# Emitting the inverses' rows later in a unit, and leaving three turns free behind the first loads of the output projection

## The chip, the cores and the metric

One core of a Trainium2 chip runs the whole program in one launch. The metric is the time on the device in microseconds (us); lower is better. The kernel before has a median of 3469.87 us over 3 runs (3465.22 to 3473.87).

## The reference

One layer of a bidirectional hybrid encoder, on 2048 tokens of width 1024 in float32. A normed input is projected; one half of the channels runs through a Mamba-2 SSD group, the other through an RWKV-7 group (8 heads of 64), both in both directions of time; the two outputs are concatenated and go through one output projection; a squared-ReLU MLP follows.

```python
proj = h @ w_in
y_ssd = ssd_bidir(...)                     # 512 channels
y_rwkv = rwkv7_bidir(...)                  # 512 channels
y = concatenate([y_ssd, y_rwkv], -1) @ w_out
...
mlp = square(relu(h @ w_fc)) @ w_proj
```

The RWKV group is a recurrence over time on a 64x64 state S of each head:

```python
s_kk = einsum('dbhvk,dbhk->dbhv', S, kk)
S = S * w + v (x) k - s_kk (x) (kk * a)    # (x): outer product
y = einsum('dbhvk,dbhk->dbhv', S, r)
```

The kernel computes it in chunks of 64 tokens. Within a chunk, the steps' dependence on each other is a triangular matrix of 64x64, and the kernel inverts it. This is the triangular inverse of the title.

## The kernel before

**Stages.** The program has three: the input projection with the preparation of both groups (to about 1040 us), the stage of the units (to about 2037 us), and the MLP. The change lies in the second alone.

**Units.** `phase_rwkv` works through 32 units. A unit is one pair of head groups at one step of time, 128 tokens of it forward and 128 backward; units with even and odd numbers belong to the two pairs of head groups, so a state waits for its own pair's unit before. The state of the recurrence goes from unit to unit through the chain: L999 multiplies on VectorE (DVE) in the preparation, in the chain the matmuls L1140, the copies L1158 (ScalarE, ACT) and L1159 (DVE), L1172 and L1169 (DVE). L1169 stands once in a unit, and the prediction counts the units in the trace from one L1169 to the next, 0 after the first.

**The jobs beside the chain.** `weave` runs the chain of unit u and, in between, a few generators for other units, each spread over a part of the unit: `prep(u+3)` over 0 to 0.3 of it, `inverse(u+2)` in 16 steps over IL to IH, `merge(u+1)` over 0.5 to 0.9, `finish(u-1)` over 0.4 to 1.0. What comes out is an order of emission. The Tile framework then schedules each engine's queue by its own model of time, with that order as the priority; the queues run in the order in which they were built.

**From prep to merge.** `prep` writes the triangular matrices to DRAM (L1040, ad<-at, on SP's queue). `inverse` loads them back in blocks of 16x16 (L1046, la<-ad), sets a unit matrix (L1049, ln), and runs 15 rows of two instructions, L1055 (ltmp<-ln,la) and L1056 (ln<-ln,ltmp). For an even-numbered unit all 15 stand on DVE, for an odd one on GpSimd (POOL). It stores the result (L1059, nd<-ln) and loads it back in another layout (L1062, ni<-nd). `merge` joins the blocks to 32x32 and 64x64: L1084, L1087, matmuls L1092, L1096, L1099, a transpose on DVE (L1103, n<-ip), copies on ACT (L1106, nm<-ip), matmuls L1112, and copies to nm again (L1124).

**The output projection as filler.** TensorE is kept busy with work from `out_pieces`, a generator. Where the chain or the merge leave TensorE waiting, `dense` adds a credit and takes pieces from the generator: a yield of DENSE is three matmuls of 128x512 (L828) and costs one credit; a yield of HELD ends the round and drops the credit left, so it is a turn in which no matmuls are put in. Up to unit 17 there are 8 such turns in a unit, and one tile of the output projection takes 8 pieces. Its first pass takes the SSD half (yS) of 16 tiles, its second the RWKV half (yR), which must wait for finished units (`FA` and `k.final`). `load` fetches a tile: h (L805), yr (L808, two buffers), scales yr on DVE in the first pass (L813), rounds it on ACT (L815, yh) and takes the rest on POOL (L817, yl). `products` runs the matmuls and adds them to h on DVE (L831 in the first pass, L833 in the second). Each tile's load is started one tile ahead.

**Norms.** `finish` normalizes the units' output (L1204 to L1240), with reciprocals on DVE (L1220).

Of the kernel before, what the change touches and what calls it, by code (L numbers as in the profile page):

```python
# [96 lines left out]
PGN = 2  # L97
PH = 0.3
ML = 0.5
IL = 0.0  # L100
KP = 0
DP = 0
PS = 0
IH = 0.4
RORD = (0, 4, 1, 5, 8, 2, 9, 6, 3, 7, 10, 11)
G0 = 2
EVB = {'u': 2, 'sg': 2, 'acc': 2, 'o': 4, 'ld': 3}
# [97 lines left out]
def ppc(k, name, j):  # L205
    c = _PP[name] + j
    return k.pp[:, c:c + 1]
# [564 lines left out]
DENSE, HELD, LAST, END = "dense", "held", "last", object()  # L772


def out_pieces(k):
# [3 lines left out]
    with ExitStack() as ctx:  # L779
# [23 lines left out]
        def load(t, ys, first):  # L803
            h = wk.tile([P, D], F32, name="h")
            nc.sync.dma_start(h, k.hD[t])  # L805
            yr = wk.tile([P, 4, P], F32, name="yr")
            for g in range(2):
                nc.sync.dma_start(yr[:, 2 * g:2 * g + 2], ys[g][:, :, P * t:P * t + P].rearrange("a p t -> p a t"))  # L808
            if first:
                rsb = wk.tile([P, 2, P], F32, name="rsb")  # L810
                nc.sync.dma_start(rsb, rsD[:, t].unsqueeze(0).broadcast_to([P, 2, P]))
                for c in range(4):
                    nc.vector.scalar_tensor_tensor(yr[:, c], yr[:, c], ppc(k, "ng", c), rsb[:, c // 2], ALU.mult, ALU.mult)  # L813
            yh = wk.tile([P, 4, P], F32R, name="yh")
            nc.scalar.copy(yh, yr)  # L815
            yl = wk.tile([P, 4, P], F32R, name="yl")
            nc.gpsimd.tensor_tensor(yl, yr, yh, ALU.subtract)  # L817
            return t, h, yh, yl

        def products(ops, first, rows=None):  # L820
            (wh, wl), (t, h, yh, yl) = k.wo, ops
            for hf in range(2):
                hs = slice(512 * hf, 512 * hf + 512)
                pt = k.psg.tile([P, 512], F32, name=k.psg_name)
                mm = [(yh, wh), (yh, wl), (yl, wh)]
                mm = [(y[:, c], w[:, c, hs]) for c in range(4) for y, w in mm]
                for i, (y, w) in enumerate(mm):
                    nc.tensor.matmul(pt, y, w, start=(i == 0), stop=(i == 11))  # L828
                    if i == 11:
                        if first:  # L830
                            nc.vector.scalar_tensor_tensor(h[:, hs], h[:, hs], ALPHA, pt, ALU.mult, ALU.add)  # L831
                        else:
                            nc.vector.tensor_tensor(h[:, hs], h[:, hs], pt, ALU.add)  # L833
                    if i + 1 in (CUTS[2 * (t % 2) + hf] if first else (3, 6, 9, 12)):
                        yield DENSE
            if rows:
                ln_apply(k, wk, h, *rows, k.eps[:, 0:1], True)
            nc.sync.dma_start(k.hD[t], h)
# [43 lines left out]
        yield  # L882
        order = [t for s in range(NT // 2, NT) for t in (NT - 1 - s, s)]
        ops = load(order[0], k.yS, True)
        for j in range(NT):
            nxt = load(order[j + 1], k.yS, True) if j + 1 < NT else None
            yield
            yield from products(ops, True)
            ops = nxt
# [36 lines left out]
def phase_rwkv(k):  # L926
    nc, tc, I = k.nc, k.tc, k.I
    with ExitStack() as ctx:
# [113 lines left out]
        def inverse(u):  # L1042

            la = sm.tile([P, 16, 16], F32, name="la")
            for q in range(2):
                nc.sync.dma_start(la[64 * q:64 * q + 64], dram(AD[u], 0, [1040, 64], [64, 16], [1, 16]))  # L1046
            ln = sm.tile([P, 8, 16], F32, name="ln")
            eng = nc.vector if SUBD and u % SUBD == 0 and u < SUBE else nc.gpsimd
            eng.tensor_copy(ln, idq)  # L1049
            tmp = sm.tile([P, 40], F32, name="ltmp")  # L1050
            for r in range(15):
                yield
                w, m = 15 - r, r // 2 + 1
                tv = tmp[:, 0:m * w].rearrange("p (m t) -> p m t", m=m)
                eng.tensor_tensor(tv, ln[:, 0:m, r:r + 1].broadcast_to([P, m, w]), la[:, r:r + 1, r + 1:16].broadcast_to([P, m, w]), ALU.mult)  # L1055
                eng.tensor_tensor(ln[:, 0:m, r + 1:16], ln[:, 0:m, r + 1:16], tv, ALU.subtract)  # L1056
            nd = k.dr.tile([64, 8, 2, 16], F32, name="nd", bufs=4)
            for q in range(2):
                nc.sync.dma_start(nd[:, :, q], ln[64 * q:64 * q + 64])  # L1059
            ni = NI[u] = sm.tile([P, 8, 16], F32, name="ni")  # L1060
            for h in range(2):
                nc.sync.dma_start(ni[hsl(h)], dram(nd, 8192 * h, [16, 64], [1024, 8], [1, 16]))  # L1062
# [187 lines left out]
        def weave(main, others):  # L1250
# [10 lines left out]
            for o in others:  # L1261
                if o[0] is not k.ssd:
                    while step(o[0], o[5]) is not END:
                        pass

        k.fill = out_pieces(k)
        k.credit = 0.0
        k.final = [0] * NT

        U = 2 * UN  # L1270
        for u in range(-AH, U):
# [8 lines left out]
            if 0 <= u + AH - 1 < U:  # L1280
                jobs.append((inverse(u + AH - 1), 16, IL, IH, PI))
            if u + AH < U:
# [212 lines left out]
```

## Time and profile before

| | us |
|---|---|
| median of 3 runs (lowest to highest) | 3469.87 (3465.22 to 3473.87) |
| profiled execution | 3477.84 |
| its span in the trace | 3476.0 |
| TensorE busy in it | 3162.8 (91%) |
| VectorE | 2035.9 (59%) |
| ScalarE | 1240.3 (36%) |
| GpSimd | 975.8 (28%) |
| mean granted TensorE clock | 0.936 |

How to read it: the shares are means over three stages with different limits. Below, PE is TensorE, PEld its weight loads, DVE VectorE, ACT ScalarE, POOL GpSimd, SP the engine whose queue issues the DMAs (SPq). The granted clock is the part of full speed at which TensorE was let run. A row of the timeline gives start, duration, engine, line, operation, out<-in and shape, and in brackets the idle time just ahead of it and what ended it.

### The profile page before, as it was taken

What the parts mean: (1) busy time and instruction counts of PE and PEld (TensorE: products, weight loads), DVE (VectorE), ACT (ScalarE), POOL (GpSimd) and SP (SyncE); (2) the same over time, 40 slices, a digit from 0 to 9 for tenths busy, and PEclk for the clock granted to TensorE, in tenths of its full rate; (3) what the DMA queues carried; (4) which work ended last, traced back from release to release, by engine and by line L of the source; (5) the groups of instructions that cost most, each with busy time, mean ns of one, the idle gap of its engine ahead of it and who ended that gap; (6) DMA issues with size and microseconds to landing.
All of it is one profiled execution on the core that took longest, in us unless ns stands there. A gap on an engine that the chain in (4) does not pass through costs nothing.

```text
span 3476.0 us, 62902 instructions
## 1 busy us (share of the span) xinstructions
PE 3162.8 (91%) x24551; PEld 2525.6 (73%) x24551; DVE 2035.9 (59%) x4186; ACT 1240.3 (36%) x2574; POOL 975.8 (28%) x1278
## 2 busy tenths in 40 slices
PE   5879989988876888888898889999999999999998
PEld 4767867766765666666666678888888788888886
DVE  7798457767675666565767554444444664444446
ACT  3556323433335454455655531122222222222221
POOL 0352134444553221223454551111111111111113
PEclk9989999999995899986978999999999999999999
DMA  5345356776777666656665552111111331111111
GB/s 206 132 158 179 122 148 190 210 214 189 214 226 198 158 170 157 161 158 171 171 164 156 151 189 91 49 49 46 47 49 49 103 109 49 49 49 49 49 49 61
DMA packets 630137, 446.70 MB, mean 129 GB/s; under 512 B 193456, under 2 KB 553552, under 8 KB 629840
## 3 DMA queue, kind: packets, MB, share of 16 engines
q1 hardware_dynamic: 629840, 442.69, 43.5%
q8 instruction: 193, 3.16, 0.4%
q14 instruction: 104, 0.85, 0.1%
HBM read 295.43 MB, written 147.14 MB: 127 GB/s over the span
## 4 chain that ended last, share of the span: by engine, by line
PE 58%; DMA 13%; DVE 13%; issue 4%; POOL 3%; SPq 2%; ACT 2%; DVEq 0%; POOLq 0%; ACTq 0%
PE ps L1362 7%; PE ps L1363 7%; PE ps L1364 7%; PE ps L1384 6%; PE ps L1382 6%; PE ps L1383 6%; PE psg L828 3%; DMA R<-rows 2%; PE psg L268 2%; PE psg L269 2%; PE psg L270 2%; PE ch L1140 2%; DMA la<-ad 1%; DMA ad<-at 1%; PE ps L1009 1%
## 5 line engine op out<-in xcount | busy, mean ns | idle before, releaser
L1388 DVE TENSOR_TENSOR acc<-acc,ps 128x512 f32<-128x512 f32 x464 | 318.2, 687 | 445.3 <-PE ps L1384 443.0
L1369 POOL TENSOR_TENSOR ul<-r,uh 128x512 fp32r<-128x512 f32 x128 | 171.1, 1338 | 1189.6 <-ACT uh L1368 1189.6
L1364 PE MATMUL ps<-hl,fh 128*128 128x512 f32 x1024 | 401.6, 392 | 0.0
L1363 PE MATMUL ps<-hh,fl 128*128 128x512 f32 x1024 | 401.5, 392 | 0.0
L1362 PE MATMUL ps<-hh,fh 128*128 128x512 f32 x1024 | 397.5, 393 | 0.6 <-DVE h L833 0.4
L1384 PE MATMUL ps<-ph,ul 128*128 128x512 f32 x1008 | 393.3, 390 | 0.0
L1383 PE MATMUL ps<-pl,uh 128*128 128x512 f32 x1008 | 393.0, 390 | 0.0
L1382 PE MATMUL ps<-ph,uh 128*128 128x512 f32 x1008 | 392.8, 390 | 0.0
L268 PE MATMUL psg<-hh,wh 128*128 128x512 f32 x864 | 357.2, 414 | 9.7 <-ACT u L287 8.9
L269 PE MATMUL psg<-hh,wl 128*128 128x512 f32 x864 | 354.8, 411 | 0.0
L270 PE MATMUL psg<-hl,wh 128*128 128x512 f32 x864 | 352.6, 409 | 1.4 <-DVE hl L238 1.4
L1350 ACT CAST ph<-wraw 128x1024 fp32r<-128x1024 f32 x63 | 63.3, 1051 | 531.2 <-PE ps L1384 527.8
L1362 PEld LDWEIGHTS ps<-hh,fh 128*128 128x128 f32 x1024 | 192.1, 188 | 43.6 <-DVE h L833 0.9
L1363 PEld LDWEIGHTS ps<-hh,fl 128*128 128x128 f32 x1024 | 192.3, 188 | 42.6
L1364 PEld LDWEIGHTS ps<-hl,fh 128*128 128x128 f32 x1024 | 192.2, 188 | 42.7
L1383 PEld LDWEIGHTS ps<-pl,uh 128*128 128x128 f32 x1008 | 189.4, 188 | 40.9
L1382 PEld LDWEIGHTS ps<-ph,uh 128*128 128x128 f32 x1008 | 189.1, 188 | 40.8
L1384 PEld LDWEIGHTS ps<-ph,ul 128*128 128x128 f32 x1008 | 189.3, 188 | 40.4
L268 PEld LDWEIGHTS psg<-hh,wh 128*128 128x128 f32 x864 | 169.5, 196 | 49.1 <-ACT u L287 10.1
L270 PEld LDWEIGHTS psg<-hl,wh 128*128 128x128 f32 x864 | 168.4, 195 | 39.6 <-issue 3.2
L269 PEld LDWEIGHTS psg<-hh,wl 128*128 128x128 f32 x864 | 169.3, 196 | 35.7 <-issue 2.3
L1366 ACT ACTIVATE r<-ps 128x512 f32<-128x512 f32 x128 | 76.8, 601 | 291.3 <-PE ps L1364 286.5
(294 smaller groups left out, 6182.6 us busy)
## 6 DMA issues: line engine op xcount, KB each, us to landing
h<-hD SPq DMA_DIRECT2D x64, 512.0 KB, 3.8
wraw<-in_w_fc_dram SPq DMA_DIRECT2D x64, 512.0 KB, 3.9
wraw<-in_w_proj_dram SPq DMA_DIRECT2D x64, 512.0 KB, 4.4
rk<-rk SPq DMA_DIRECT2D x64, 384.0 KB, 4.4
eD<-et SPq DMA_DIRECT2D x32, 514.0 KB, 2.7
E<-eD SPq DMA_DIRECT2D x64, 257.0 KB, 4.4
xs<-xg SPq DMA_DIRECT2D x64, 256.0 KB, 4.1
R<-rows SPq DMA_DIRECT2D x64, 256.0 KB, 4.4
```

The lines of the kernel that those rows point to most:

```text
L268: nc.tensor.matmul(pt, wh[:, c], hh[:, c], start=(c == 0), stop=False)
L269: nc.tensor.matmul(pt, wl[:, c], hh[:, c], start=False, stop=False)
L270: nc.tensor.matmul(pt, wh[:, c], hl[:, c], start=False, stop=(c == KC - 1))
L828: nc.tensor.matmul(pt, y, w, start=(i == 0), stop=(i == 11))
L1362: nc.tensor.matmul(pt, wh[:, c], k.hh[:, c, ns], start=(c == 0), stop=False)
L1363: nc.tensor.matmul(pt, wl[:, c], k.hh[:, c, ns], start=False, stop=False)
L1364: nc.tensor.matmul(pt, wh[:, c], k.hl[:, c, ns], start=False, stop=(c == KC - 1))
L1369: nc.gpsimd.tensor_tensor(ul[:, ns], r, uh[:, ns], ALU.subtract)
L1382: nc.tensor.matmul(pt, uh[:, ts], ph[:, hs], start=(i == 0), stop=False)
L1383: nc.tensor.matmul(pt, uh[:, ts], pl[:, hs], start=False, stop=False)
L1384: nc.tensor.matmul(pt, ul[:, ts], ph[:, hs], start=False, stop=(i == len(ops) - 1))
L1388: nc.vector.tensor_tensor(acc[j][:, hs], acc[j][:, hs], pt, ALU.add)
```

## The change

Two constants say over which part of a unit the rows of an inverse are emitted, IL and IH. They go from 0.0 and 0.4 to 0.25 and 0.7. And in `out_pieces`, behind the loads of the first tile of the first pass, three HELD yields are put in, so three turns pass without matmuls, and all of the first pass comes three turns (three eighths of a unit) later against the chain. Numbers, shapes and engines of instructions stay; their order changes. Behind the new lines, line numbers are 2 higher (L1055 is L1057).

```diff
-IL = 0.0
+IL = 0.25
...
-IH = 0.4
+IH = 0.7
...
         ops = load(order[0], k.yS, True)
+        for _ in range(3):
+            yield HELD
         for j in range(NT):
```

What the built queues show, at three places. First the steady part of the first pass. DVE's queue in a unit whose rows stand on DVE, before, from the multiplies L999 on (L1084 is the first step of the next merge):

```order
L999 TENSOR_TENSOR kr<-rk,E 128x2x128 x4
L1055 TENSOR_TENSOR ltmp<-ln,la 128x15
L831 SCALAR_TENSOR_TENSOR h<-h,psg 128x512
L1056 TENSOR_TENSOR ln<-ln,ltmp 128x15
L1055 TENSOR_TENSOR ltmp<-ln,la 128x14
L1103 STREAM_TRANSPOSE n_13436<-ip 128x256
L1056 TENSOR_TENSOR ln<-ln,ltmp 128x14
L1084 TENSOR_TENSOR dd<-ni,rc 128x256
L1055 TENSOR_TENSOR ltmp<-ln,la 128x26
L1056 TENSOR_TENSOR ln<-ln,ltmp 128x2x13
L1055 TENSOR_TENSOR ltmp<-ln,la 128x24
```

And after:

```order
L1001 TENSOR_TENSOR kr<-rk,E 128x2x128 x4
L1057 TENSOR_TENSOR ltmp<-ln,la 128x15
L1058 TENSOR_TENSOR ln<-ln,ltmp 128x15
L1057 TENSOR_TENSOR ltmp<-ln,la 128x14
L1058 TENSOR_TENSOR ln<-ln,ltmp 128x14
L1057 TENSOR_TENSOR ltmp<-ln,la 128x26
L1105 STREAM_TRANSPOSE n_13398<-ip 128x256
L1086 TENSOR_TENSOR dd<-ni,rc 128x256
L1058 TENSOR_TENSOR ln<-ln,ltmp 128x2x13
L1057 TENSOR_TENSOR ltmp<-ln,la 128x24
L1058 TENSOR_TENSOR ln<-ln,ltmp 128x2x12
```

The first row stands directly behind the multiplies in both; h's accumulation L831 leaves its place behind the first row, and the transpose (L1103, now L1105) comes one row step later.

The end of the same rows on DVE, before, from the addition L831 on:

```order
L831 SCALAR_TENSOR_TENSOR h<-h,psg 128x512
L1056 TENSOR_TENSOR ln<-ln,ltmp 128x5x6
L1016 TENSOR_TENSOR ra<-ps,rc 128x4x64 x2
L997 TENSOR_TENSOR bk<-bk_13962,E 128x2x128 x2
L1055 TENSOR_TENSOR ltmp<-ln,la 128x30
L1056 TENSOR_TENSOR ln<-ln,ltmp 128x6x5
L1055 TENSOR_TENSOR ltmp<-ln,la 128x24
L1056 TENSOR_TENSOR ln<-ln,ltmp 128x6x4
L1055 TENSOR_TENSOR ltmp<-ln,la 128x21
L1056 TENSOR_TENSOR ln<-ln,ltmp 128x7x3
L1055 TENSOR_TENSOR ltmp<-ln,la 128x14
```

And after, where the same stretch holds yr (L813):

```order
L1018 TENSOR_TENSOR ra<-ps,rc 128x4x64 x2
L1058 TENSOR_TENSOR ln<-ln,ltmp 128x6x4
L1057 TENSOR_TENSOR ltmp<-ln,la 128x21
L1058 TENSOR_TENSOR ln<-ln,ltmp 128x7x3
L813 SCALAR_TENSOR_TENSOR yr<-yr,pp,rsb 128x128 x2
L1057 TENSOR_TENSOR ltmp<-ln,la 128x14
L813 SCALAR_TENSOR_TENSOR yr<-yr,pp,rsb 128x128 x2
L1058 TENSOR_TENSOR ln<-ln,ltmp 128x7x2
L999 TENSOR_TENSOR bk<-bk_13943,E 128x2x128 x2
L1057 TENSOR_TENSOR ltmp<-ln,la 128x8
L1058 TENSOR_TENSOR ln<-ln,ltmp 128x8
```

yr stood beside the rows 7 and 8 before, further up; it stands around row 14 now, and fewer rows are left behind L997 (now L999).

In the unit beside it, whose rows stand on POOL, POOL's queue before:

```order
L1081 TENSOR_TENSOR ao<-at,rc 128x512
L1055 TENSOR_TENSOR ltmp<-ln,la 128x15
L817 TENSOR_TENSOR yl<-yr,yh 128x512
L1056 TENSOR_TENSOR ln<-ln,ltmp 128x15
L1055 TENSOR_TENSOR ltmp<-ln,la 128x14
L1056 TENSOR_TENSOR ln<-ln,ltmp 128x14
```

And after, at the rows' end:

```order
L1057 TENSOR_TENSOR ltmp<-ln,la 128x21
L1058 TENSOR_TENSOR ln<-ln,ltmp 128x7x3
L817 TENSOR_TENSOR yl<-yr,yh 128x512
L1057 TENSOR_TENSOR ltmp<-ln,la 128x14
L1058 TENSOR_TENSOR ln<-ln,ltmp 128x7x2
L1057 TENSOR_TENSOR ltmp<-ln,la 128x8
L1058 TENSOR_TENSOR ln<-ln,ltmp 128x8
L1051 COPY ln<-rc 128x128
```

yl (L817) has moved from inside the first row to behind the thirteenth; the rows keep their order.

The second place is ACT's queue in unit 18, before:

```order
L1015 COPY at<-ps 64x256 x2
L1025 COPY bkt<-ps 128x4x64
L1149 ACTIVATE rs<-ch 128x256
L815 CAST yh<-yr 128x512 x2
L1124 COPY nm_9566<-ip 32x8x32 x2
L1025 COPY bkt<-ps 128x4x64
L1036 COPY zv<-ps 64x2x64 x4
```

And after:

```order
L1212 COPY ya<-ps 128x256
L1214 ACTIVATE sq<-ps 128x256
L1126 COPY nm_9566<-ip 32x8x32 x2
L1220 ACTIVATE sd<-ps,eps 128x256
L1212 COPY ya<-ps 128x256
```

The copies of nm (L1124, now L1126) stood behind two casts of yh (L815). The same two casts come after them now, at the start of unit 19:

```order
L1017 COPY at<-ps 64x256 x2
L1027 COPY bkt<-ps 128x4x64
L815 CAST yh<-yr 128x512 x2
L1027 COPY bkt<-ps 128x4x64
L1038 COPY zv<-ps 64x2x64 x4
```

The third is DVE's queue in unit 27, before, up to the chain's copy L1159:

```order
L1055 TENSOR_TENSOR ltmp<-ln,la 128x14
L1056 TENSOR_TENSOR ln<-ln,ltmp 128x14
L1055 TENSOR_TENSOR ltmp<-ln,la 128x26
L1056 TENSOR_TENSOR ln<-ln,ltmp 128x2x13
L999 TENSOR_TENSOR kr<-rk,E 128x2x128 x2
L1055 TENSOR_TENSOR ltmp<-ln,la 128x24
L999 TENSOR_TENSOR kr<-rk,E 128x2x128 x2
L1056 TENSOR_TENSOR ln<-ln,ltmp 128x2x12
L1087 STREAM_TRANSPOSE n_22630<-dd 128x256
L1055 TENSOR_TENSOR ltmp<-ln,la 128x33
L1220 RECIPROCAL sd<-sd 128x128 x2
L1159 COPY zv<-ch 64x4x64
```

And after, up to the same copy (L1161):

```order
L1001 TENSOR_TENSOR kr<-rk,E 128x2x128 x4
L1057 TENSOR_TENSOR ltmp<-ln,la 128x15
L1058 TENSOR_TENSOR ln<-ln,ltmp 128x15
L1222 RECIPROCAL sd<-sd 128x128 x2
L1057 TENSOR_TENSOR ltmp<-ln,la 128x14
L1089 STREAM_TRANSPOSE n_22610<-dd 128x256
L1231 TENSOR_TENSOR ya<-ya,sd 128x256
L833 TENSOR_TENSOR h<-h,psg 128x512
L1058 TENSOR_TENSOR ln<-ln,ltmp 128x14
L1161 COPY zv<-ch 64x4x64
```

Before, two pairs of reciprocals (the first is some rows further up, behind L1169) and five rows begin ahead of the copy; after, one pair and two rows, and an accumulation L833.

## The prediction

> **What bounds the kernel now.** I read the page first: its span, and the row of the granted TensorE clock, which falls below 9 tenths in the middle of the program alone.
>
> ```profile
> span 3476.0 us, 62902 instructions
> PEclk9989999999995899986978999999999999999999
> ```
>
> Then the windows by stage. The columns are: the window, its length, then the busy time with the instruction count of PE, PEld, DVE, ACT and POOL, then the granted clock, the DMA share and GB/s.
>
> ```profile
> 1240.00:1440.00 200.00, 175.00 (x3329) 135.69 (x3328) 126.08 (x398) 98.28 (x281) 50.55 (x140) 0.93 0.63 163
> 1440.00:1640.00 200.00, 172.23 (x3036) 134.16 (x3035) 113.82 (x329) 106.75 (x297) 70.15 (x160) 0.82 0.65 172
> 1640.00:1840.00 200.00, 179.62 (x2923) 135.11 (x2923) 146.99 (x376) 115.73 (x317) 95.57 (x170) 0.86 0.63 162
> 1840.00:2040.00 200.00, 163.49 (x2315) 123.86 (x2314) 131.96 (x273) 99.41 (x244) 106.63 (x157) 0.87 0.58 170
> 2040.00:3476.00 1436.00, 1419.61 (x6231) 1163.95 (x6229) 654.56 (x870) 303.34 (x421) 211.19 (x151) 1.00 0.19 61
> ```
>
> From 2040 us on, TensorE is busy for 1419.6 of 1436.0 us at clock 1.00: that is the MLP, which the change does not touch. What can move lies ahead of it, in the stage of the 32 units. There no engine is full: TensorE stands for 200.00 − 175.00 = 25 us of the first window, and its clock is 0.93 to 0.82. So waits set that stage, and the waits between 1240 and 2000 us come next (in total, times, longest).
>
> ```profile
> DVE ltmp L1055 <- DMA la<-ad: 36.6, 9, 6.2
> PE ip L1112 <- ACT nm L1106: 34.0, 10, 5.6
> POOL ltmp L1055 <- DMA la<-ad: 55.1, 12, 9.5
> ```
>
> The first row of an inverse (L1055) waits for its loads on DVE and on POOL alike, and the merge's matmul L1112 waits nearly as long. The timeline of two units shows that these are one thing (start, duration, engine, line; in brackets the idle time before and what ended it).
>
> ```profile
> 1294.65 0.21 POOL L1055 TENSOR_TENSOR ltmp<-ln,la 128x15 f32<-128x15 f32 x1 [3.44 <-DMA la<-ad]
> ...
> 1305.36 0.21 POOL L1056 TENSOR_TENSOR ln<-ln,ltmp 128x8 f32<-128x8 f32 x1
> ...
> 1307.37 0.55 SPq L1059 DMA_DIRECT2D nd<-ln  x1
> ...
> 1317.59 1.32 SPq L1046 DMA_DIRECT2D la<-ad  x2
> ...
> 1321.93 0.17 DVE L1055 TENSOR_TENSOR ltmp<-ln,la 128x15 f32<-128x15 f32 x1 [6.21 <-DMA la<-ad]
> ...
> 1322.91 0.44 DVE L1103 STREAM_TRANSPOSE n<-ip 128x256 f32<-128x256 f32 x1
> ...
> 1324.93 1.06 PE L1112 MATMUL ip<-n,at 32*32 32x32 f32 x32 [5.61 <-ACT nm L1106]
> ...
> 1335.83 0.17 DVE L1056 TENSOR_TENSOR ln<-ln,ltmp 128x8 f32<-128x8 f32 x1
> ...
> 1336.03 1.22 SPq L1059 DMA_DIRECT2D nd<-ln  x2
> ...
> 1346.82 0.21 POOL L1055 TENSOR_TENSOR ltmp<-ln,la 128x15 f32<-128x15 f32 x1 [3.75 <-DMA la<-ad]
> ```
>
> It is a ring: POOL's rows, their store (nd), the next inverse's loads (la), which stand behind that store in SP's queue, DVE's rows, their store, the loads, POOL's rows again. One turn takes 1346.82 − 1294.65 = 52.17 us: 27.3 from POOL's first row to DVE's (1294.65 to 1321.93), 13.9 for DVE's rows among its other work (to 1335.83), 11.0 for store and loads (to 1346.82). DVE stands 6.21 us at its first row, and behind it in the same queue stands the merge's transpose L1103, so TensorE stands 5.61 us at L1112.
>
> **What the change does to the ring.** In the order of DVE's queue the first row stays where it was, directly behind the four L999 multiplies, in every steady unit; only the later rows move back. SP's queue keeps its order too: store, then loads. So neither the 6.21 us nor L1103 behind it goes, and the 27.3 and 11.0 us stay. What is left is the 13.9 us, in which DVE has work ready.
>
> There the matter is yr (L813). POOL's yl (L817), which frees the buffer of the next yr load, moves from the first rows to behind the thirteenth.
>
> ```profile
> 1296.02 1.27 POOL L817 TENSOR_TENSOR yl<-yr,yh 128x512 fp32r<-128x512 f32 x1
> ...
> 1301.41 1.26 DVE L813 SCALAR_TENSOR_TENSOR yr<-yr,pp,rsb 128x128 f32<-128x128 f32 x4 [3.61 <-POOL ln L1056]
> 1302.59 0.41 DVE L1172 TENSOR_TENSOR zt<-zz,ch 128x256 f32<-128x256 f32 x1
> ```
>
> Thirteen of the fifteen rows, which take 10.9 us from 1294.65 to 1305.57, end at about 1304.1 and put yl about 8 us later, and yr follows yl by 1301.41 − 1296.02 = 5.4 us. In the unit whose rows are on POOL, L1172 now stands ahead of yr, and the 3.61 us no longer hold it; but DVE has 6.21 us to spare at its next first row, so nothing is gained or lost. In the unit with rows on DVE, yr now stands around row 14, where its load may be late and holds the rows' end and the store. Below: nothing, since yr comes as much later in DVE's queue as its load does in SP's. Above: 1.2 us, one such yr step, in each turn. I take +0.6 in each of the five turns that run whole between 1240 and 1500 us: **+3 us (0 to +6)**. The three free turns put one more triple of out-projection matmuls under the 5.61-us stall and take it from elsewhere: no time, since the ring does not wait for TensorE.
>
> **Unit 18.** Here the out-projection's second pass begins, and a cast of a late load stands ahead of the merge on ACT.
>
> ```profile
> 1603.00 0.42 DVE L1169 TENSOR_TENSOR zz<-zz,ch 128x256 f32<-128x256 f32 x1
> ...
> 1629.28 1.14 ACT L815 CAST yh<-yr 128x512 fp32r<-128x512 f32 x2 [6.04 <-DMA yr<-yR]
> 1630.32 0.74 ACT L1124 COPY nm<-ip 32x256 f32<-32x256 f32 x2
> 1630.73 1.29 PE L1140 MATMUL ch<-rs,nm 64*64 64x64 f32 x14 [3.38 <-ACT nm L1124]
> ...
> 1639.82 0.42 DVE L1169 TENSOR_TENSOR zz<-zz,ch 128x256 f32<-128x256 f32 x1
> ...
> 1670.93 0.42 DVE L1169 TENSOR_TENSOR zz<-zz,ch 128x256 f32<-128x256 f32 x1
> ```
>
> From one L1169 to the next this unit takes 36.8 us and the next one 31.1. After the change L1124 stands ahead of the cast, and the 6.04 + 1.14 us of load and cast leave the chain. Bounds: nothing (the tiles behind it come too late) to 7.2; I take **−6**, which makes the unit as long as its neighbour.
>
> **Unit 19.** DVE's transpose L1103 now stands behind eleven rows, where it stood behind eight: three rows at about 0.5 us, read from the next row, are +1.6.
>
> ```profile
> 1650.73 0.89 PE L1112 MATMUL ip<-n,at 32*32 32x32 f32 x32 [1.92 <-ACT nm L1106]
> ```
>
> That wait of 1.92 becomes 3.5. I take **+2**; bounds 0, and +10 if it draws a stretch at half clock as in the next part.
>
> **Unit 27.** The two clock rows are windows of 7.00 and 27.70 us.
>
> ```profile
> 1323.00:1330.00 7.00, 5.07 (x59) 3.97 (x60) 5.55 (x25) 3.36 (x10) 0.00 (x0) 0.52 0.72 227
> 1893.00:1920.70 27.70, 24.08 (x265) 18.17 (x265) 14.97 (x45) 8.52 (x26) 7.34 (x14) 0.51 0.43 106
> ```
> ```profile
> 1878.86 0.42 DVE L1169 TENSOR_TENSOR zz<-zz,ch 128x256 f32<-128x256 f32 x1
> ...
> 1888.96 0.35 ACT L1158 COPY zv<-ch 64x256 f32<-64x256 f32 x1
> ...
> 1893.44 1.75 DVE L1220 RECIPROCAL sd<-sd 128x128 f32<-128x128 f32 x2
> 1895.22 0.43 DVE L1159 COPY zv<-ch 64x256 f32<-64x256 f32 x1
> 1895.70 1.12 PE L1140 MATMUL ch<-zv,bkt 128*64 128x64 f32 x16 [3.65 <-DVE zv L1159]
> ...
> 1918.38 0.42 DVE L1169 TENSOR_TENSOR zz<-zz,ch 128x256 f32<-128x256 f32 x1
> ```
>
> Two pairs of reciprocals stand ahead of L1159 in this unit, and TensorE waits 3.65 us for it though ACT's half was done 5.9 us earlier. Behind that stall the clock is 0.51 for 27.7 us, and the unit takes 39.5 us. After the change one pair of the two is behind L1159, and three of the rows that stood ahead, while one h accumulation comes ahead of it: 1.75 us and more, so the stall comes to under 2 us. If the half-clock stretch goes with it, 27.7 × 0.49 = 13.6 us of it go at most; if another stall draws it, nothing. I take three quarters, **−10**. In the Trainium skill, "TensorE: Matmul & The Clock Gate", Part 1, "What's actually happening", the array goes to half rate after an idle window of about 3.4 us and comes back after about 3.4 us of sustained work. This trace agrees on the start (3.65 us idle, then 0.51) and not on the end: TensorE was busy 24.08 of 27.70 us and stayed slow. By that rule the stretch would cost some 2 us and the term would be an estimated −4 in place of −10.
>
> **Sum.** +3 − 6 + 2 − 10 = −11 us. The profiled execution took 3477.84 us, 8 above the median of 3469.87; the edit is put on the median: 3469.87 − 11 = **3459 us**. Other units change by single steps in both directions, which I leave at nothing. A difference of 0.3%, 10.4 us, is about what a measurement of this kernel tells from none; the forecast is just past it.
>
> **The rivals.** *No change.* The ring keeps its 52 us, and in the second half the time taken out of units 18 and 27 comes back at the next wait: the la loads still hold both engines there (POOL's longest wait for them, 9.5 us, is above). Half the gain or less: 3465 to 3473. For it: the rows' front end does not move at all, so in the steady units the change does not do what it says. Against it: the two long units have causes that the order removes.
>
> *Slower, by the yr load.* The place is DVE's rows in the first pass. yl is 8 us later, the yr load behind it, and the next yh and yl with it. If in the unit with DVE's rows yr stands 4 us rather than 0.6 for its load, the row end, the store, and every later la go back by 4 us a turn; seven turns until the first pass ends make 28 us, and 28 + 2 − 16 = +14: 3484. It decides from (16 − 2) ÷ 7 = 2 us of wait a turn. For it: the 3.61-us wait ahead of yr today. Against it: yr itself moved back past six rows and L1172.
>
> *Faster, by the clock.* A triple of matmuls in the stall shortens it by about 0.8 us; the stalls at L1112 have a mean of 34.0 ÷ 10 = 3.4 us, so half of them would fall under 3.4 and leave the clock up. Each window of 7 us at 0.52 costs 7 × 0.48 = 3.4 us; four of them 14: 3459 − 14 = 3445. By the page just named such stalls are too short for an idle window. Against it: the ring waits for loads, not for TensorE, so a faster clock only lengthens the stall.
>
> **How the numbers follow.** The forecast has 0.45. Its own range runs from 3449 (ring and unit 19 at nothing, unit 18 at −7.2, unit 27 at −13.6: −20.8) to 3469 (unit 27 at nothing); unit 18 and the most of unit 27 have to come in to pass 0.3%, and I give 0.33 to that and 0.12 to less. By the clock 0.08, so faster 0.41. No change 0.20, so within 0.3% 0.32. Slower 0.27: the yr load 0.20, unit 19 at half clock 0.07. The range leaves out the outer ends of the clock's and the yr load's cases: 3440 to 3482.
>
> **What would show it.** Right: DVE's wait on la before L1055 stays at 5 to 6 us a turn and the turns at 52 to 53 us; unit 18 takes about 31 us; unit 27 about 29, with no half clock behind its L1159. Wrong: turns of 55 us or more with a wait before L813; turns under 50; a half-clock stretch in unit 27 all the same, or a new one behind unit 19's L1112.

## The result, and the profile after

The changed kernel takes 3499.36 us in the median of 6 runs (3489.21 to 3510.08). The kernel before took 3478.76 in its 6 runs by now (3465.22 to 3494.34; the three that were known ahead had 3469.87). The ratio on record is 1.0074, with a 95% interval of 1.0047 to 1.0102 (the two medians alone give 1.0059): slower, where the forecast was faster, and outside the range of 3440 to 3482. Its profiled execution took 3495.88 us, with a mean clock of 0.933.

The page of the profile after, the same two lines:

```profile
span 3494.1 us, 62872 instructions
PEclk9989999999886889898889989999999999999999
```

The windows between 1240 and 1540 us, where only the first pass runs: first the two profiles of the kernel before (a second one was taken later), then the two of the kernel after. The last three columns are the granted clock, the DMA share and GB/s.

```profile
1240.00:1540.00 300.00, 261.40 (x4997) 202.44 (x4997) 186.07 (x585) 147.33 (x420) 76.51 (x210) 0.93 0.62 159
1240.00:1540.00 300.00, 269.55 (x4929) 208.37 (x4923) 189.42 (x583) 145.39 (x419) 72.37 (x196) 0.89 0.61 156
...
1240.00:1540.00 300.00, 268.04 (x4618) 206.02 (x4618) 174.78 (x527) 135.47 (x391) 73.83 (x206) 0.87 0.58 146
1240.00:1540.00 300.00, 272.48 (x4725) 209.97 (x4725) 181.81 (x551) 138.52 (x400) 71.36 (x191) 0.87 0.59 151
```

In the same 300 us TensorE ran 4618 and 4725 matmuls after the change, and 4997 and 4929 before: in the mean it does 6% less while it is as busy. DVE's waits between 1240 and 1500 us (in total, times, longest) keep their head, and the second line after was far down before. The first two lines are those of before:

```profile
DVE ltmp L1055 <- DMA la<-ad: 26.4, 5, 6.2
DVE kr L1014 <- PE ps L1009: 5.2, 10, 0.9
...
DVE ltmp L1057 <- DMA la<-ad: 30.9, 5, 7.1
DVE kr L1016 <- PE ps L1011: 17.9, 11, 4.8
```

One turn of the ring after the change, from POOL's first row to the next:

```profile
1354.14 0.21 POOL L1057 TENSOR_TENSOR ltmp<-ln,la 128x15 f32<-128x15 f32 x1 [5.51 <-DMA la<-ad]
...
1381.54 0.17 DVE L1057 TENSOR_TENSOR ltmp<-ln,la 128x15 f32<-128x15 f32 x1 [5.16 <-DMA la<-ad]
...
1394.71 0.17 DVE L1058 TENSOR_TENSOR ln<-ln,ltmp 128x8 f32<-128x8 f32 x1
...
1395.68 1.58 SPq L1061 DMA_DIRECT2D nd<-ln  x2
1397.47 3.49 SPq L1042 DMA_DIRECT2D ad<-at  x2
...
1402.55 1.27 SPq L1064 DMA_DIRECT2D ni<-nd  x2
1403.91 0.58 SPq L991 DMA_DIRECT2D bk<-bk  x1
1404.59 1.30 SPq L1048 DMA_DIRECT2D la<-ad  x2
...
1408.82 0.21 POOL L1057 TENSOR_TENSOR ltmp<-ln,la 128x15 f32<-128x15 f32 x1 [6.31 <-DMA la<-ad]
```

The turn takes 1408.82 − 1354.14 = 54.7 us in place of 52.2. DVE's rows are not longer (13.3 us from 1381.54 to 1394.88). What is longer is the way from the rows' end to POOL's first row: 13.9 us in place of 10.8 (1336.00 to 1346.82). The store nd is issued 0.8 us behind the rows' end, and 0.03 before. Then the two ad stores take 3.49 us to issue, and 1.27 before; the load ni, which reads nd back, stands behind them in SP's queue and comes 7.7 us behind the rows' end, and 3.8 before:

```profile
1337.34 1.27 SPq L1040 DMA_DIRECT2D ad<-at  x2
...
1339.78 1.28 SPq L1062 DMA_DIRECT2D ni<-nd  x2
...
1342.90 1.30 SPq L1046 DMA_DIRECT2D la<-ad  x2
```

The chain of work that ended last runs here through the store nd (start, length):

```profile
1396.28 6.21 DMA nd<-ln
```

It ends at 1402.49, and ni is issued at 1402.55. la follows behind ni and one bk load; ad had landed 1.35 us before la was issued, at 1403.24.

Where all of it went is read from L1169 (L1171), which stands once in a unit. The stretches run from one unit's L1169 to another's; the last column of stretches goes to the MLP's first matmul, and the MLP takes 1430 us in each of these profiles.

| us | start of unit 0 | units 0 to 3 | 4 to 15 | 16 to 27 | 28 to 30 | 31 to the MLP | span |
|---|---|---|---|---|---|---|---|
| before | 1124.5 | 114.9 | 307.0 | 372.0 | 59.3 | 68.0 | 3476.0 |
| before, second profile | 1121.0 | 109.1 | 309.6 | 363.8 | 62.9 | 71.2 | 3467.8 |
| after | 1121.8 | 112.5 | 336.3 | 355.6 | 68.6 | 69.1 | 3494.1 |
| after, second profile | 1117.8 | 111.6 | 331.9 | 364.4 | 72.3 | 68.2 | 3496.3 |

Units 4 to 15, six turns of the ring, take 308.3 us in the mean of the two profiles before and 334.1 after: +25.8, or 51.4 and 55.7 us a turn. This is the loss. Units 16 to 27 gain 7.9, units 28 to 30 lose 9.3, and the rest gives 4; the spans differ by 23.3.

### The profile page after: what moved, and what is told of

It reads as the page before. It is cut to its first block, busy times and chain, and to the rows that moved or that the text cites. A ratio compares the mean times of both kernels' runs of the same rounds, so it can differ in the third digit from the quotient of the medians.

```text
span 3494.1 us, 62872 instructions
## 1 busy us (share of the span) xinstructions
PE 3190.8 (91%) x24551; PEld 2547.3 (73%) x24551; DVE 2048.0 (59%) x4186; ACT 1234.8 (35%) x2574; POOL 977.2 (28%) x1278
## 4 chain that ended last, share of the span: by engine, by line
PE 50%; DMA 8%; DVE 6%; SPq 2%; ACT 2%; issue 2%; POOL 2%; DVEq 0%; POOLq 0%; ACTq 0%
PE ps L1364 7%; PE ps L1365 7%; PE ps L1366 7%; PE ps L1386 6%; PE ps L1384 6%; PE ps L1385 6%; PE psg L828 3%; PE ch L1142 2%; DMA la<-ad 1%; DMA nd<-ln 1%; PE ps L1011 1%; DMA ad<-at 1%; PE yp L1157 1%; DVE ln L1058 1%; DVE ltmp L1057 1%
## 5 line engine op out<-in xcount | busy, mean ns | idle before, releaser
L268 PEld LDWEIGHTS psg<-hh,wh 128*128 128x128 f32 x864 | 170.1, 197 | 50.3 <-ACT u L287 10.6
L269 PEld LDWEIGHTS psg<-hh,wl 128*128 128x128 f32 x864 | 170.0, 197 | 35.7 <-issue 2.0
```

The costliest lines, as they stand in the source:

```text
L268: nc.tensor.matmul(pt, wh[:, c], hh[:, c], start=(c == 0), stop=False)
L269: nc.tensor.matmul(pt, wl[:, c], hh[:, c], start=False, stop=False)
```

## The experiments

Theory A was the rival of the prediction, turned a little: yr (L813) and its wait stand ahead of the multiply bk (L997) on DVE, and bk leads over L1009 and the matrices at to ad and the next la. Theory B: the loads of yr, ya and h are now issued just ahead of the store nd, and delay it. Each run below is compared with runs of the kernel before on the same chip. A turn is a sixth of the time of units 4 to 15.

**The two parts apart.** First the constants of the rows alone:

```diff
-IL = 0.0
+IL = 0.25
...
-IH = 0.4
+IH = 0.7
```

> The kernel before with the rows' constants alone (0.25 and 0.7), no free turns. In units 5 to 16 its queues read as before's. Theory A (yr, L813, now stands ahead of the multiply bk, L997, on DVE, and bk feeds ad and the next la): turns of the ring stay at 52 us, total within 0.4% of before, from the second half alone. Theory B (the loads of yr, ya and h are now issued just ahead of the store nd and delay it): the same. If the rows' later emission itself were the loss: turns of 55 us, total up 0.7%.

Measured: ratio 1.0050 (1.0033 to 1.0067), 3487.24 us against 3472.56; turns of 51.0 us. The ring is untouched by the rows' constants, as the built order had said. Its total missed what was expected: units 16 to 27 took 382.4 us, 10 to 19 more than in the two profiles of before, and units 0 to 3 took 2 to 8 less.

Then the three free turns alone:

```diff
+        for _ in range(3): yield HELD
```

> The kernel before with the three free turns alone. Theories A and B: turns of 55 us between units 5 and 16, as after the whole change, so 20 to 30 us more there than before; total +0.4 to +0.9%. If the rows were the loss: turns of 52 us and a total like before's.

Measured: 1.0089 (1.0066 to 1.0112), turns of 56.0 us. The turns make the loss in the ring, and all of it.

**Other numbers of free turns.** Five and seven, without the rows' constants (`range(5)`, `range(7)`):

> As the turns alone, but five free turns in place of three. yr then stands behind the first bk of a unit, while SP issues yr, ya and h still just ahead of the store nd in units with rows on POOL. Theory A: turns of 52 to 53 us, total within 0.3% of before. Theory B: turns of 55 us, total +0.4 to +0.9%.

Measured: 1.0087 (1.0064 to 1.0110), turns of 54.8 us. These are the figures of theory B, and not by its way: from DVE's rows to POOL's the turn takes 11.5 us in the mean, about as before, and DVE's rows take 16.7 us in place of 14.1 to 14.4. yr is not the reason. Over these rows it waits 0.4 us in all, and it stands among them before as well. But in the first four of the six turns all four multiplies L999 and a second pair of L1014 stand among the rows, where there are none of L999 and one pair before: in the turn from 1312.70 us these take 0.76, 0.75 and 0.88 us.

> As the turns alone, but seven free turns. yr stands at the end and the start of units, behind both bk of the unit before; SP issues yr directly ahead of nd in units with rows on DVE. Theory A: turns of 52 us or less (down to 50), total at before's or up to 0.6% below. Theory B: turns of 54 us, total +0.3 to +0.7%.

Measured: 1.0049 (1.0034 to 1.0065), turns of 51.9 us. So the loss does not come with free turns as such; it depends on where in a unit they put the pieces. That is theory A's turn and not B's; A's total missed, and B's came.

**yr taken out.** The scaling of yr is left out of the kernel before and of the three turns alone:

```diff
-                for c in range(4):
+                for c in range(4 * 0):
                     nc.vector.scalar_tensor_tensor(yr[:, c], yr[:, c], ppc(k, "ng", c), rsb[:, c // 2], ALU.mult, ALU.mult)
```

> The kernel before without the scaling of yr (the four L813 of each tile of the first pass and the load of rsb), so the output lacks that factor. It is the reference for the next run. Theory A and B: turns of 49 to 51 us, total 0 to 0.4% below before.

> The same without the scaling of yr, with three free turns. The order of everything else is that of the turns alone: SP still issues yr, ya and h just ahead of the store nd, and h's accumulation stands where it stood there. Theory A (the scaling and its wait stand ahead of bk): turns within 1 us of the run without turns and without scaling, total within 0.3% of it. Theory B (the loads ahead of the store): turns 3 to 5 us longer than that, total 0.5 to 0.9% above it.

Measured: without turns 1.0030 (1.0011 to 1.0049) and 50.9 us a turn, where the total was expected at before's or below; with three turns 1.0135 (1.0080 to 1.0189) and 56.9 us a turn. Theory A falls: there is no yr step on DVE, and the three turns cost 6 us a turn all the same.

**A store ahead of the store.** Theory B, put into the kernel before:

```diff
-            nd = k.dr.tile([64, 8, 2, 16], F32, name="nd", bufs=4)
+            nd = k.dr.tile([64, 8, 2, 16], F32, name="nd", bufs=4); nc.sync.dma_start(k.dr.tile([P, 8, 128], F32, name="dum", bufs=4), ln.rearrange("p a b -> p (a b)").unsqueeze(1).broadcast_to([P, 8, 128]))
```

> The kernel before with one more transfer of 512 KB, a store that repeats an inverse's rows eight times into unused DRAM, on SP directly ahead of each store nd. Theory A: one more issue of 0.6 us in front of nd, turns of 52 to 53.5 us, total +0.1 to +0.4%. Theory B: nd lands 1 to 3 us later in both halves of a turn, turns of 54 to 57 us, total +0.5 to +1.2%.

Measured: 1.0065 (1.0041 to 1.0088), turns of 52.1 us: theory B's total and theory A's turn. The DMA issues between 1230 and 1540 us tell what it did to the store (count, KB each, median us from issue to landing): before, after, and this run.

```profile
nd<-ln SPq DMA_DIRECT2D x24, 32.0 KB, 3.2
...
nd<-ln SPq DMA_DIRECT2D x22, 32.0 KB, 4.6
...
nd<-ln SPq DMA_DIRECT2D x24, 32.0 KB, 4.4
```

The added store makes nd land about as late as the change does: 4.4 us, where the change has 4.6 and 4.4 and the two profiles of before 3.2 and 3.7. The turn is 0.7 us longer than the mean of before (52.1 − 51.4), but that is not the whole price of a late nd. POOL's rows took 9.9 us here and 10.9 and 11.1 before, so the edit moved other work too; from rows to rows the two halves of a turn lose 1.1 and 0.5 us. And in four of its six DVE halves (the way from DVE's rows to POOL's) in the table below, one of the two la loads is issued ahead of ni, so that only the other stands behind it. Theory B is true of the store; what it costs in the changed kernel this run does not tell.

**The order on TensorE.** What the two runs with three turns share with the changed kernel, and no other run has, is found on TensorE: the preparation's second L1009 of a unit. Before, its 16 records stand in one piece; after, chain work stands between its halves.

```profile
1335.08 1.16 PE L1009 MATMUL ps<-kr,bk 64*128 64x128 f32 x16
```

```profile
1393.61 1.16 PE L1011 MATMUL ps<-kr,bk 64*128 64x128 f32 x8
1394.70 0.68 PE L1157 MATMUL yp<-kr,zv 64*64 64x64 f32 x16
1395.21 0.28 PE L1142 MATMUL ch<-rs,nm 64*64 64x64 f32 x2
1395.42 0.82 PE L1011 MATMUL ps<-kr,bk 64*128 64x128 f32 x5
```

The last of L1009 ends 1.2 us after the first began in the upper fence, 2.9 in the lower one, where three more records follow at 1396.08, 1396.19 and 1396.30. ACT copies the matrices at from it, one piece before, two after:

```profile
1336.75 0.87 ACT L1015 COPY at<-ps 64x256 f32<-64x256 f32 x2 [0.43 <-DVE kr L1014]
```

```profile
1397.08 0.36 ACT L1017 COPY at<-ps 64x256 f32<-64x256 f32 x1
1397.73 0.37 ACT L1017 COPY at<-ps 64x256 f32<-64x256 f32 x1
```

They end 1.6 us after the rows' end before (1337.62 and 1336.00) and 3.2 us after it here (1398.10 and 1394.88). This is theory D: the split makes at late, and with it ad and la. In this very turn it does not decide: la stood behind ni, and ni waited for nd, as shown above. Where the clock is at half over it, as in this turn of the kernel after (its window 1282 to 1289 us has a clock of 0.50), L1009 takes 5.3 us and DVE waits 4.83:

```profile
1282.91 2.07 PE L1011 MATMUL ps<-kr,bk 64*128 64x128 f32 x8
1286.16 1.43 PE L1011 MATMUL ps<-kr,bk 64*128 64x128 f32 x5
1287.60 0.63 PE L1011 MATMUL ps<-kr,bk 64*128 64x128 f32 x2
```

```profile
1288.27 0.88 DVE L1016 TENSOR_TENSOR kr<-ps,rc 64x256 f32<-64x256 f32 x2 [4.83 <-PE ps L1011]
```

To undo the split, L1009 gets priority, in the whole change and in the kernel before.

```diff
-nc.tensor.matmul(gps[h][:, pr, c], ...)
+with tc.high_priority(offset=1000): nc.tensor.matmul(gps[h][:, pr, c], ...)
```

> The whole change, with the preparation's matmuls L1009 given priority, so that the second eight of a unit stand in one piece on TensorE again (three free turns had put the last four of them behind the chain's L1155 and L1140). The triple that three turns put ahead of L1112 stays there, and so do the loads ahead of the store nd and yr (half of it) ahead of other work. Theory D (the split delays the matrices at, their store ad and the next la): turns of 51 to 53 us, total within 0.3% of before. Theory B (loads ahead of the store) and any theory of the triple's place: turns stay at 55 to 57 us, total +0.5 to +0.9%.

> The kernel before with the same priority for L1009, as the reference: it was in one piece there already, and its first eight move ahead. All theories: turns of 50 to 52 us, total within 0.4% of before.

Measured: 1.0205 (1.0180 to 1.0231) with turns of 57.6 us, and 1.0147 (1.0105 to 1.0189) with 55.5. Neither is what theory D expected. The priority moves the first L1009 as well and costs 4 us a turn by itself, so only the two can be compared. Over units 4 to 15 they differ by 2.1 us a turn, but the reference has one long unit there (unit 15, 38.5 us); over the turns of the table below they differ by 3.3 us (57.7 and 54.4, from the same profiles). So most of the loss stays with L1009 in one piece. The trace of the changed kernel with priority shows why: in all six of its DVE halves ni is issued within 0.1 us of nd's landing, 6.8 us behind the rows' end in the mean, and la goes out behind it. nd is late there without any split.

**The same kernels again.**

> The whole change once more, for a second profile. All theories: turns of 55 to 57 us between units 5 and 16. What the units 16 to 28 take (355.6 us in the first profile) shows how far that figure belongs to the kernel or to the execution: within 5 us if to the kernel.

> The kernel before once more, for a second profile. All theories: turns of 51 to 52 us; units 16 to 28 took 372.0 us in the first profile, and within 5 us of that again if the figure belongs to the kernel.

Measured: 1.0078 (1.0055 to 1.0102) and 0.9998 (0.9977 to 1.0019). The turns repeat within 0.8 us (56.1 and 55.3 after, 51.2 and 51.6 before). Units 16 to 27 repeat within 8 to 9 us, not 5 (355.6 and 364.4; 372.0 and 363.8). So what a single profile shows there, such as the 382.4 of the rows alone, is only partly the kernel's.

**Numbers of turns that leave L1009 whole.** In the built queues, two and six free turns move yr, yl and the loads too, but not L1009.

> The whole change with two free turns in place of three. In its queues L1009's second eight stand in one piece and the second triple stands behind L1112 again, as before; yr stands ahead of bk (as with none), yl behind the eighth row, and the yr and h loads directly ahead of nd in units with rows on POOL. Theory D (the split on TensorE is most of the loss): turns of 51 to 52.5 us, ad issued about 3 us behind the rows' end on DVE. Theory B: about 1 us more. If three turns lose time for another reason that grows with their number: turns of 54 us. Total by D: within 0.4% of before.

Measured: 1.0070 (1.0046 to 1.0094), turns of 52.1 us. In this run nd and the last row read:

```profile
1389.70 0.17 DVE L1056 TENSOR_TENSOR ln<-ln,ltmp 128x8 f32<-128x8 f32 x1
...
1389.90 1.22 SPq L1059 DMA_DIRECT2D nd<-ln  x2
1391.22 2.28 SPq L1040 DMA_DIRECT2D ad<-at  x2
...
1395.96 1.29 SPq L1046 DMA_DIRECT2D la<-ad  x2
```

la follows the rows' end by 6.1 us; in the turns shown above it was 6.9 before and 9.7 after. The turn lies in theory D's range, and in theory B's (about 1 us more) as well: in this run's DVE half SP issues just ahead of nd what it did before, and ni comes 3.9 us behind the rows' end, so both late links are gone from it. On POOL, where the loads stand ahead of nd, the way from rows to rows is 0.9 us longer than before. The total is as neither has it: units 16 to 27 took 385.0 us.

> The whole change with six free turns. On TensorE the steady order is that of before word for word, and yr stands behind the preparation's work on DVE and at a unit's start. Theory D: turns of 50.5 to 52.5 us, ad issued about 3 us behind the rows' end on DVE; total -0.4% to +0.3%. If the loss grows with the number of turns: turns over 55 us.

> Six free turns alone, with the rows' constants of before; between units 5 and 16 its order is that of the run with rows and six turns. Theory D: the same turns as there, within 0.5 us; total -0.3% to +0.5%, the rest from the second half.

Measured: 1.0074 (1.0048 to 1.0100) with turns of 54.8 us, and 1.0066 (1.0044 to 1.0088) with 55.0. Here theory D misses, with TensorE's order that of before. SP's queue has the reason. In the half behind POOL's rows:

```profile
1420.55 0.97 SPq L808 DMA_DIRECT2D yr<-yS  x2
1421.61 0.42 SPq L805 DMA_DIRECT2D h<-hD  x1
1422.12 1.28 SPq L1040 DMA_DIRECT2D ad<-at  x2
...
1428.56 1.30 SPq L1046 DMA_DIRECT2D la<-ad  x2
```

With six turns the loads of yr and h are issued directly ahead of ad, and la, which waits for ad, follows it by 6.4 us. ad's median landing in that window is 5.5 us, where it was 3.1 before:

```profile
ad<-at SPq DMA_DIRECT2D x24, 128.0 KB, 3.1
...
ad<-at SPq DMA_DIRECT2D x22, 128.0 KB, 5.5
```

In the half behind DVE's rows it is nd again: ni is issued 7.7 us behind the rows' end, where it was 4.4 before, and la behind it, with L1009 in one piece and ad early. That the landings make up the loss is read from these rows; it was not tried by itself.

The table has means over the turns whose first row lies between 1225 and 1540 us: us from an inverse's last row to the end of the next issue of ad, to the next issue of ni, and to the next inverse's first row, on DVE and on POOL.

| kernel | L1009 | turn | DVE: ad | DVE: ni | DVE: next row | POOL: ad | POOL: next row |
|---|---|---|---|---|---|---|---|
| before (two profiles) | whole | 51.2, 51.6 | 2.9, 2.9 | 4.4, 4.4 | 11.2, 10.7 | 7.7, 7.9 | 15.1, 15.4 |
| rows alone | whole | 51.0 | 3.0 | 4.2 | 11.0 | 8.0 | 15.1 |
| rows, two turns | whole | 52.1 | 3.0 | 3.9 | 10.6 | 9.4 | 16.1 |
| after (two profiles) | split | 56.1, 55.3 | 6.5, 5.9 | 6.8, 5.9 | 13.7, 13.1 | 10.2, 9.4 | 17.3, 16.5 |
| three turns alone | split | 56.0 | 6.2 | 6.8 | 13.4 | 9.7 | 17.0 |
| three turns, no yr | split | 56.9 | 7.7 | 5.3 | 14.2 | 10.0 | 16.7 |
| five turns | whole | 54.8 | 2.0 | 5.7 | 11.5 | 8.0 | 14.8 |
| six turns | whole | 55.0 | 4.4 | 7.7 | 13.4 | 8.3 | 18.8 |
| seven turns | whole | 51.9 | 3.1 | 5.1 | 11.4 | 8.7 | 16.7 |
| store ahead of nd | whole | 52.1 | 4.0 | 6.8 | 12.0 | 9.2 | 15.7 |
| after, L1009 with priority | whole | 57.6 | 4.5 | 6.8 | 13.1 | 9.5 | 17.8 |
| before, L1009 with priority | whole | 55.5 | 4.5 | 3.6 | 11.9 | 8.3 | 15.6 |

In the column "DVE: ad" the four split profiles have 5.9 to 7.7 us, and the whole ones 2.0 to 4.5. But a split is not needed for a long DVE half: six turns and the kernel after with priority take 13.4 and 13.1 us with ad at 4.4 and 4.5 us and ni late, at 7.7 and 6.8. The other way round, three turns without yr take 14.2 us with the latest ad, at 7.7, and ni at 5.3. So a long DVE half goes with either link being late, and in the kernel after both are. In all 12 DVE halves of the two profiles of before ni is issued within 0.1 us of nd's landing, and la behind it, when ad has landed already. In 5 of the 11 after it is still so; in 4 the issue or the landing of ad releases ni or la; in 2 the trace does not tell.

In the kernel after, the DVE half of a turn loses 2.4 us (13.4 − 11.0) by the two links together, and no run gives their shares. The POOL half loses 1.6 (16.9 − 15.2, unrounded). There ad stands behind ni in SP's queue, and ni waits for nd, which is issued 1.8 and 2.0 us behind POOL's last row in place of 0.0, since the loads of yr and h, with two stores of yaD between and behind them, stand directly ahead of it:

```profile
1364.03 0.99 SPq L808 DMA_DIRECT2D yr<-yS  x2
1364.83 0.21 POOL L1058 TENSOR_TENSOR ln<-ln,ltmp 128x8 f32<-128x8 f32 x1
1365.62 0.42 SPq L805 DMA_DIRECT2D h<-hD  x1
1366.64 1.31 SPq L1061 DMA_DIRECT2D nd<-ln  x2
```

That part is theory B's. The two halves sum to 4.1 of the 4.3.

**The whole change with seven turns.**

> The whole change with seven free turns in place of three. Its order between units 5 and 16 is that of the seven turns alone, whose turns took 51.9 us. Theories A and B: turns of 52 us; total 0 to 0.5% above before, as the parts alone, if the second half does not change by more than 10 us.

Measured: 1.0004 (0.9980 to 1.0028), 3470.31 us against 3472.04; turns of 52.6 us, units 16 to 27 in 358.3. It is the best of the changed kernels, and does not beat the kernel before. The rows' constants alone and the seven turns alone cost 0.5% each; together they cost nothing that can be told from noise, so the parts do not add up.

## Why the prediction was wrong

*The ring (+3 us forecast, +25.8 measured).* The step that failed is "SP's queue keeps its order too: store, then loads", with what was drawn from it, that the 27.3 and 11.0 us of a turn stay. Store and ring loads kept their order, but the loads of yr and h, which the three turns move, came closer ahead of the store nd (in the turns shown h is issued 1.0 us ahead of it behind POOL's rows and 3.9 us behind DVE's, where it was 4.7 and 10.0 before). nd lands later behind the rows, and ni, which stands ahead of la in the same queue, waits for nd. ni is issued 6.4 us behind DVE's rows in place of 4.4, and the way from DVE's rows to POOL's takes 13.4 us in place of 11.0; from POOL's rows to DVE's it takes 16.9 in place of 15.2. A second step failed with it: "no time, since the ring does not wait for TensorE", said of the triple that the three turns move. The new order on TensorE splits L1009, which makes at and ad late, and ad holds ni or la in 4 of the 11 DVE halves. In the trace of before that link was off the end of the chain by little: at was ready about when nd had been issued. An unchanged order of two entries does not fix when a queue reaches them, nor when they have their data. What stands around nd in SP's queue, and the order on TensorE, where the split is plain, were not weighed.

*The rival of yr.* It had the sign, a time of 3484 and the right stage, and not the cause: without yr's scaling the loss stays.

*Unit 18 (−6) and unit 27 (−10).* Right in mechanism, and the first too small. Unit 18 took 24.7 and 27.0 us in the two profiles after, against 36.8 and 38.0. In the first of them ACT's copies of nm wait 0.35 us for TensorE alone, and the cast comes after them:

```profile
1635.51 0.73 ACT L1126 COPY nm<-ip 32x256 f32<-32x256 f32 x2 [0.35 <-PE ip L1122]
```

Unit 27 took 27.8 and 29.2 against 39.5 and 35.7, with this wait in place of the 3.65 us, where the forecast had under 2:

```profile
1912.05 1.12 PE L1142 MATMUL ch<-zv,bkt 128*64 128x64 f32 x16 [2.79 <-DVE zv L1161]
...
1912.00:1926.00 14.00, 13.96 (x196) 11.56 (x196) 12.53 (x43) 6.30 (x20) 3.78 (x6) 0.89 0.63 185
```

Behind it the clock is 0.50 from 1912 to 1915 us and 1.00 from there to 1926: a short stretch at half clock is left of the long one. In the second profile after, the wait is 1.76 us, and the clock is 0.99 and more until 1918 us. The Trainium skill gives, in "TensorE: Matmul & The Clock Gate", Part 1, "What's actually happening", an idle window of about 3.4 us ahead of half rate. Here 2.79 us had one behind it too.

*Unit 19 (+2).* It took 36.9 and 36.2 us against 31.1 and 34.2: +3.9 in the mean.

*The sum of the second half.* These three units come to −16.8 us in the means of two profiles (25.8 − 37.4, 28.5 − 37.6, 36.6 − 32.7, unrounded). All of units 16 to 27 give only −7.9, and units 28 to 30 lose 9.3: what the long units gained was given back by others, as the no-change rival had it for this part. Why the last units are longer after the change was not tried; with the turns alone they took 58.1, with the rows alone 64.3, so neither part by itself shows the 68.6 and 72.3.

*The clock.* The rival by the clock did not come: the clock between 1240 and 1540 us fell from 0.93 and 0.89 to 0.87 and 0.87. That is no cause of the longer turns by itself either, since the two profiles of before differ by 0.04 in the clock and by 0.4 us in the turn.

*Left open.* Why the rows' constants alone make the kernel 0.5% slower: the built order puts no change of theirs into units 5 to 16, and units 16 to 27 took 10 to 19 us longer in the one profile, where two profiles of one kernel differ by 8 to 9. And neither the split nor the loads ahead of nd were undone by themselves: each edit that took one away moved other work as well, so how the 2.4 us of the DVE half divide between them is open. Why nd lands later was not tried beyond the added store.

## What to carry to other kernels

A ring of waits is only as fixed as its second-latest link: before a stretch of it is called unchanged, list for each wait what else it waits for, how late that is, and what stands ahead of it in its queue. When one late link is found, look whether another would hold the same instruction without it. Filler work for an engine that "has time" is moved into the way of whatever shares its queue, so read the filled engine's order around each short instruction that a transfer waits for. And a shift of a periodic filler has to be tried at each phase: here 0, 2, 3, 5, 6 and 7 turns gave 51 to 56 us a turn with different losers, and no trend.

## What the runs showed of the hardware that was not expected

What large transfer stands ahead of a small store in one DMA queue goes with when the store lands. With a store of 512 KB put ahead of nd, nd's median landing was 4.4 us, where two profiles without it had 3.2 and 3.7. With yr and h (128 KB twice and 512 KB) directly ahead of ad in the half behind POOL's rows, ad's over both halves was 5.5 us, where it was 3.1 before; other work was moved in that kernel too.

Two executions of one kernel differed by 12 us of full clock within the same 300 us (0.93 and 0.89 of the clock lose 21 and 33 us of it) and took the same time a turn within 0.4 us.
